# Small matmuls of a hybrid SSD and attention block, put into tiles of the TensorE array

## The chip, the cores and the metric

The kernel runs on one core of one Trainium2 chip. The metric is the time of one execution in microseconds on the device. The kernel before takes 2657.98 us, the median of three runs (2657.9 to 2659.08).

The core's engines run side by side, each through its own list of instructions: TensorE (PE; its weight loads are listed apart as PEld), VectorE (DVE), ScalarE (ACT), GpSimd (POOL) and SyncE (SP), which issues the DMAs. TensorE multiplies a stationary operand of up to 128 rows by 128 columns with a moving one; the product lands in a bank of PSUM. An operand that lies on a part of the 128 partitions uses a part of the array's rows, and an output on a part of the partitions uses a part of its columns.

## The reference

The reference is two blocks of a network, one behind the other. The first (token mixers and a mixture of experts) isn't touched. The second takes 256 tokens with 16 meta tokens ahead of them, 272 in all, through two layers. Cut to what the change touches:

```python
def ssd_mixer(...):                         # 32 heads of 64, 8 groups
    ...
    y = ssd_chunked(xs, dt, a_log, bm, cm) + xs * d_skip[:, None]
    y = y.reshape(bsz, L, D_INNER) * jax.nn.silu(z)
    y = rms_norm(y.reshape(bsz, L, SSD_GROUPS, ...), norm_g...)   # mean square of each of 8 groups
...
def sliding_window_attention(q, k, v, q_norm_g, k_norm_g, sinks):
    q = rotary(rms_norm(q, q_norm_g), pos)  # 16 query heads of 64
    k = rotary(rms_norm(k, k_norm_g), pos)  # 4 key heads
    ...
    probs = jax.nn.softmax(jnp.concatenate([s_meta, s_band, sink], axis=-1), axis=-1)
...
for l in range(2):
    proj = rms_norm(h, norm1_g[l]) @ w_in[l]
    z, xbc, dt_raw, q, k, v, gate_logits = jnp.split(proj, ...)
    y_ssd, y_attn = ssd_mixer(...), sliding_window_attention(...)
    merged = g_ssd * (y_ssd @ w_ssd_down[l]) + g_attn * (y_attn @ w_attn_down[l])
    h = h + merged @ w_o[l]
    h = h + square(relu(rms_norm(h, norm2_g[l]) @ w_mlp_up[l])) @ w_mlp_down[l]
```

## The kernel before

All activations of the second block lie with features on partitions and the 272 tokens along the free dimension; tile kinds `U` (8 x 272 columns) and `Z` (4 x 272) hold them. The last layer drops the 16 meta tokens from its outputs, so there a tile has 256 columns (`n0` is 16) in most places.

`dense` (L1374) multiplies a weight slice of 512 columns by the activations. It loads 1 MB of weights, and for each 256 columns ScalarE casts them into a tile `Y` of the rounded type (the high part) and VectorE subtracts that from the weights into another `Y` (the low part); six `Y` buffers stand in a ring. Three matmuls for each product (high by high, high by low, low by high) go into one of four PSUM banks `pd`; these are the rows `pd<-U,Y` of the profile. Everything else that TensorE does writes one of four banks `pq`, in plain fp32. `evac` reads the banks when the sums are done.

In a layer the order is: B, C, x and z projections, and behind each pair of x and z slices two groups of the SSD (`ssd_group`, L1654, eight groups); the mean squares of y; the k, v and q projections; attention (L1732); then the projections down, the gates, and the MLP. This is the order of the program's text. A scheduler then lays the instructions of each engine in one row, by priority and by its own estimate of when operands are ready: that is how dense matmuls of later projections come to stand between the small ones.

The small matmuls that the change touches:

- **Mean squares** (`stat`, L1493). ScalarE squares a tile of 128 features into one of five buffers `r1`, and a matmul with a table of constants (`sh`, `sy`) of 28 columns adds the sums of one tile into its rows of a 28-row bank. `stat_y` does this for the 16 tiles of y in two halves, `ev_qkv` (L1562) for 2 tiles of k and 8 of q, column by column as `dense` hands them over. `stats` (L1505) makes inverse roots of the 28 rows.
- **Gain rows** (`ynorm`, L1513). A matmul with a column of the identity spreads one of the 28 rows over 128 partitions; four for each half of y.
- **Meta rows of the SSD** (L1711). The 16 meta tokens act on all tokens. For each head a matmul of 16 rows (`xm`, the meta tokens' x by their step, made by ScalarE at L1697) and 64 output columns starts the sum that two matmuls of the masked products (`sg`, `xd`) go on with.
- **Scores** (L1784). For each of 16 heads up to three matmuls: 128 queries by 272 keys, 128 by 144 and, in layer 0, 16 by 16. A head lies on 64 of 128 partitions: even heads in the lower half, odd heads in the upper. Keys that lie in the other half are taken from a swapped copy (`ksw`, tile name `cr`, L1756). Behind each matmul VectorE scales, masks and takes the maximum (L1785); ScalarE takes the exponentials, VectorE divides (L1798 on), three transposes through TensorE follow (L187, operand `cb`), and ScalarE copies their bank into `pT`. Four heads share a transposed tile of meta columns and the products with v (L1816 on).

Of the kernel before, what the change touches and what calls it, by code (L numbers as in the profile page):

```python
# [17 lines left out]
P = 128  # L18
# [18 lines left out]
for _n, _w in (("cos", 272), ("sin", 272), ("cm", 656), ("am", 432), ("perm", 128),  # L37
               ("hsel", 128), ("e16", 16), ("sh", 54), ("sy", 55)):
    C2[_n] = (_o, _o + _w)
    _o += _w  # L40
# [3 lines left out]
def const_tables():  # L44
# [68 lines left out]
    sh, sy = np.zeros((P, 54), f), np.zeros((P, 55), f)  # L113
# [1176 lines left out]
class Block2:  # L1290
# [8 lines left out]

    def c(self, n):  # L1300
        a, b = C2[n]
        return self.cst[:, a:b]
# [71 lines left out]
    def dense(self, w, cols, xh, xl, n0, evac, nk=8, pairs=False):  # L1374
# [6 lines left out]
        for q0 in range(0, nk, 4):  # L1381
# [5 lines left out]
            for c0 in range(0, npc, 256):  # L1387
# [5 lines left out]
                for m, c in enumerate(cols):  # L1393
                    if not (c0 <= c.start - a < c1):
                        continue
                    s = slice(c.start - a - c0, c.stop - a - c0)
                    o = ps[m][: c.stop - c.start, n0:L2]
                    for q in range(4):
                        kk = q0 + q
                        k.mm3(o, hi[:, q, s], lo[:, q, s], xh(kk)[:, n0:], xl(kk)[:, n0:], kk == 0, kk == nk - 1)  # L1400
        if pairs:
# [26 lines left out]
    def layer(self, l, h, n0, r1=None):  # L1428
# [64 lines left out]
        def stat(ps, src, w, first, last, n1):  # L1493
            sq = self.tl([P, L2], "r1", 5)
            k.act(sq[:, n1:], src, AF.Square)
            k.mm(ps[:28, n1:L2], w, sq[:, n1:], start=first, stop=last)

        def stat_y(hf):
            if hf == 0:
                self.ys = k.pq()  # L1500
            for t in range(8):
                g = 20 + 4 * hf + t // 2
                stat(self.ys, xs[hf][:, t, n0:], self.c("sy")[:, 27 - g : 55 - g], hf == 0 and t == 0, hf == 1 and t == 7, n0)

        def stats(ps, n1):  # L1505
            rs, v = self.row()[:28], self.tl([P, L2], "r1", 5)[:28]
            k.ts(v[:, n1:], ps[:28, n1:L2], EPS, ALU.add)
            self.rsqrt(rs[:, n1:], v[:, n1:], [28, L2 - n1])
            return rs
# [3 lines left out]
        def ynorm(hf, rs):  # L1513
# [48 lines left out]
        def ev_qkv(b, n1):  # L1562
            def f(m, ps):
                k.acopy(qkv[b][:, m, n1:], ps[:, n1:])
                if b < 2 or m < 2:
                    if not qs:
                        qs.append(k.pq())
                    r = 8 * b + 2 * m
                    stat(qs[0], ps[:, n1:], self.c("sh")[:, 26 - r : 54 - r], b == 2 and m == 0, b == 1 and m == 3, n1)
                    self.rotary(qkv[b][:, m], prm["qg"] if b < 2 else prm["kg"], prm["qgp"] if b < 2 else prm["kgp"], n1)  # L1570
# [3 lines left out]
        self.dense(w_in, self.cols(7200, 512), xh, xl, 0, ev_qkv(2, 0))  # L1574
        for j in range(2):
            self.dense(w_in, self.cols(6176 + 512 * j, 512), xh, xl, n0, ev_qkv(j, n0))
# [77 lines left out]
    def ssd_group(self, g, B, C, xsv, zt, tk, cs, ncs, ncm, cs_d, prm, n0):  # L1654
# [31 lines left out]
        xm = self.tl([P, 64], "xm", 2)  # L1686
        for j in range(2):
# [34 lines left out]
    def rotary(self, x, g, gp, n0):  # L1722

        k = self.k
        ps = k.pq()
        k.mm(ps[:, n0:L2], self.c("perm"), x[:, n0:])
        t = self.tl([P, L2], "r1", 5)
        k.stt(t[:, n0:], ps[:, n0:L2], gp, self.c("sin")[:, n0:], ALU.mult, ALU.mult)
        k.stt(x[:, n0:], x[:, n0:], g, self.c("cos")[:, n0:], ALU.mult, ALU.mult)
        k.add(x[:, n0:], x[:, n0:], t[:, n0:])  # L1730

    def attention(self, qkv, oh, ol, rs, prm, n0):  # L1732
# [9 lines left out]
        for i, (a, n) in enumerate(tiles):  # L1742
            k.tr(sp[:n, i * 16 : i * 16 + 16], rs[0:16, a : a + n])
        k.ts(qc[:, :32], sp[:, :32], 0.125, ALU.mult)
        if n0 == 0:
            k.ts(qc[:16, 32:48], sp[:16, 32:48], 0.125, ALU.mult)

        kr = [k.pq(), k.pq()]
        for j in range(2):
            for e in range(2):  # L1750
                r = 16 + 2 * j + e
                k.mm(kr[j][64 * e : 64 * e + 64, :L2], k.ident[0:28, r : r + 1].to_broadcast([28, 64]), rs)
# [17 lines left out]
        for kh in range(4):  # L1770
# [3 lines left out]
            for r in range(4):  # L1774
                hq = 4 * kh + r
                pr, e = hq // 2, hq % 2
                rows = slice(64 * e, 64 * e + 64)
                kt = qt(8 + kh // 2)[:] if kh % 2 == e else ksw[:, kh // 2]
                sp = k.pq()
                lg = self.tl([P, 432], "cb", 2)  # L1780
                mx, su, es = (self.tl([P, 3], f"at{x}", 3) for x in range(3))
                for i, (a, n) in enumerate(tiles):
                    o, nk = geo[i]
                    k.mm(sp[:n, o : o + nk], qt(pr)[rows, a : a + n], kt[rows, 0:nk])  # L1784
                    V.tensor_tensor_reduce(out=lg[:n, o : o + nk], in0=sp[:n, o : o + nk], in1=am[:n, o : o + nk],  # L1785
                                           scale=qc[:n, i * 16 + hq : i * 16 + hq + 1], scalar=prm["sink"][:n, hq : hq + 1],
                                           op0=ALU.add, op1=ALU.max, accum_out=mx[:n, i : i + 1])
                parts = ((P, slice(0, 2)),) + (((16, slice(2, 3)),) if n0 == 0 else ())
                for n, c in parts:
                    k.ts(mx[:n, c], mx[:n, c], -1.0, ALU.mult)  # L1790
                    k.act(es[:n, c], mx[:n, c], AF.Exp, bias=prm["sink"][:n, hq : hq + 1])
                for i, (a, n) in enumerate(tiles):
                    o, nk = geo[i]
                    k.act(lg[:n, o : o + nk], lg[:n, o : o + nk], AF.Exp, bias=mx[:n, i : i + 1], accum_out=su[:n, i : i + 1])
                for n, c in parts:
                    k.add(su[:n, c], su[:n, c], es[:n, c])
                    V.reciprocal(su[:n, c], su[:n, c])
                t2 = k.pq()  # L1798
                for i, (a, n) in enumerate(tiles):
                    o, nk = geo[i]  # L1800
                    k.ts(lgm[:n, i, 32 * r : 32 * r + 16], lg[:n, o : o + 16], su[:n, i : i + 1], ALU.mult)
                    if i < 2:
                        k.ts(lg[:n, o + 16 : o + nk], lg[:n, o + 16 : o + nk], su[:n, i : i + 1], ALU.mult)
                        k.tr(t2[:, a - 16 : a - 16 + n], lg[:n, o + 16 : o + 144])
                    if i < 1:
                        k.tr(t2[:, 256:384], lg[:n, o + 144 : o + 272])
                pT = self.tl([P, 384], "pT", 4)
                k.acopy(pT, t2[:, 0:384])
# [152 lines left out]
```

## Time and profile before

| | before |
|---|---|
| median of the runs | 2657.98 us |
| the profiled execution's own time | 2663.16 us |
| its span on the core | 2661.3 us |
| mean granted TensorE clock | 0.971 |
| second block in the span | about 1343 to 2661 us |
| busy: PE, PEld, DVE, ACT | 2487.2, 1786.6, 1398.3, 1068.1 us |

The predictions are made against the profiled execution. Its span is the time from the first to the last instruction on the core; the 1.9 us between span and time lie around it. Times in the trace count from the start of the span. In a row, "out<-in" names the tiles written and read, "128*64 128x272" is the shape of the stationary operand and of the moving one. Every fp32 matmul appears as two records. All matmuls have line L184 or L187 (a transpose), since helpers record them, so they are told apart by their tiles: `r,cst` are mean squares, `row,ident` gain rows, `sm,xm` meta rows, `Z,Z` and `cr,Z` scores, `ident,cb` a softmax's transposes.

### The profile page before, as it was taken

The page shows a single profiled execution, that of the slowest core. Times are in us where ns is not written, and L with a number is a line of the kernel's source. Part 1 is how long each engine was busy: PE and PEld are TensorE (multiplying, and loading weights), DVE is VectorE, ACT ScalarE, POOL GpSimd, SP SyncE. Part 2 cuts the span into 40 slices and gives each one's busy share as a digit, 9 for nine tenths or more (in the row PEclk, how much of TensorE's full clock was granted, in tenths as well). Part 3 has the DMA queues.
Part 4 walks back from the last instruction along what each step waited for, and adds up shares of the span by engine and source line. Part 5 has one row for each costly group of instructions (what it writes and reads, how often), then busy time and mean ns, then how long its engine had stood idle before and what let it go on. Part 6 is the DMA issues. An engine that isn't in the chain of part 4 may idle for free.

```text
span 2661.3 us, 38832 instructions
## 1 busy us (share of the span) xinstructions
PE 2487.2 (93%) x15461; PEld 1786.6 (67%) x15461; DVE 1398.3 (53%) x2910; ACT 1068.1 (40%) x2134; POOL 8.0 (0%) x21
## 2 busy tenths in 40 slices
PE   8979999998777999999879999999998999999999
PEld 7744333334655333333378977899998898789999
DVE  6862222221757222221287876666557887656654
ACT  3421111111532111211158755556454875555654
POOL 0000000000000000000000000000000000000000
PEclk9989999999888999999979999999999999899999
DMA  8489799998636998999855533335553553234553
GB/s 299 154 315 422 322 397 421 421 403 345 198 112 230 421 387 340 421 421 401 340 175 173 163 112 111 112 127 163 175 171 128 184 165 111 97 126 159 175 187 115
DMA packets 189788, 645.17 MB, mean 242 GB/s; under 512 B 21618, under 2 KB 35988, under 8 KB 139556
## 3 DMA queue, kind: packets, MB, share of 16 engines
q1 hardware_dynamic: 189604, 642.66, 64.6%
q8 instruction: 123, 2.02, 0.3%
q14 instruction: 61, 0.50, 0.1%
HBM read 641.49 MB, written 1.12 MB: 241 GB/s over the span
## 4 chain that ended last, share of the span: by engine, by line
PE 47%; DVE 2%; ACT 1%; issue 0%; DMA 0%; ACTq 0%; DVEq 0%
PE pd L184 38%; PE pq L184 7%; PE pq L187 1%; ACT Y L193 1%; DVE Y L196 0%; DVE r L213 0%; ACT r L190 0%; DMA cst<-in_cst 0%; DVE H L196 0%; ACT xd L193 0%; DVE r L196 0%; DVE ln_st L295 0%; DVE lnr_t L196 0%; DVE U L196 0%; DVE cb L209 0%
## 5 line engine op out<-in xcount | busy, mean ns | idle before, releaser
L184 PE MATMUL pd<-U,Y 128*128 128x272 f32 (+1 forms) x7792 | 1030.2, 290 | 15.4 <-ACT U L193 9.2
L184 PEld LDWEIGHTS pd<-U,Y 128*128 128x128 f32 x7792 | 987.2, 190 | 46.2 <-issue 22.3
L196 DVE TENSOR_TENSOR Y<-w,Y 128x1024 fp32r<-128x1024 f32 x344 | 420.1, 1222 | 248.9 <-ACT Y L193 247.4
L184 PE MATMUL pd<-w,H 128*64 128x512 f32 (+1 forms) x2112 | 502.3, 591 | 1.1 <-DMA w<-in_moe_w_up 1.1
L193 ACT CAST Y<-w 128x1024 fp32r<-128x1024 f32 x344 | 360.1, 1047 | 339.9 <-PE pd L184 300.1
L184 PEld LDWEIGHTS pd<-w,H 128*64 128x64 f32 x2112 | 155.8, 138 | 292.4 <-issue 272.0
L184 PE MATMUL pd<-w,m_hT 128*64 128x512 f32 x1040 | 232.6, 596 | 24.4 <-ACT m_hT L193 24.4
L213 DVE SCALAR_TENSOR_TENSOR t4k<-pd,m_gs,t4k 128x512 fp32r<-128x512 f32 x64 | 48.0, 751 | 272.9 <-ACT t4k L190 270.7
L184 PEld LDWEIGHTS pd<-w,m_hT 128*64 128x64 f32 x1040 | 81.5, 137 | 152.8 <-issue 120.5
L190 ACT ACTIVATE t2k<-pd 128x512 f32<-128x512 f32 (+1 forms) x37 | 21.9, 591 | 296.0 <-PE pd L184 296.0
L190 ACT ACTIVATE t4k<-pd,m_gs 128x512 fp32r<-128x512 f32 x64 | 44.0, 687 | 210.3 <-PE pd L184 193.6
L196 DVE TENSOR_TENSOR t2k<-t2k,pd 128x512 f32<-128x512 f32 (+1 forms) x33 | 22.4, 680 | 178.4 <-PE pd L184 178.4
L196 DVE TENSOR_TENSOR H<-H,pq 128x512 f32<-128x512 f32 x132 | 83.9, 681 | 52.5 <-PE pq L184 52.2
L184 PE MATMUL pd<-Xh,H 128*128 128x512 f32 (+1 forms) x320 | 105.2, 400 | 4.0 <-ACT H L193 4.0
L193 ACT COPY m_hT<-pq 128x512 f32<-128x512 f32 (+1 forms) x34 | 19.5, 573 | 218.6 <-PE pq L187 213.7
L190 ACT ACTIVATE H<-pq,m_gb 128x256 f32<-128x256 f32 (+1 forms) x136 | 64.2, 559 | 99.5 <-PE pq L184 79.0
L213 DVE SCALAR_TENSOR_TENSOR t2k<-t2k,pd 128x512 f32<-128x512 f32 (+1 forms) x33 | 22.4, 678 | 150.5 <-ACT t2k L190 150.5
L213 DVE SCALAR_TENSOR_TENSOR r<-pd,cw,r 128x270 f32<-128x270 f32 (+1 forms) x192 | 87.9, 492 | 3.7 <-ACT r L190 2.1
L184 PEld LDWEIGHTS pq<-m_P,H 128*128 128x128 f32 x544 | 73.0, 206 | 25.1 <-issue 19.5
L184 PEld LDWEIGHTS pq<-t4k,m_pgT 128*128 128x128 f32 x256 | 43.7, 188 | 64.9 <-ACT t4k L190 20.3
L184 PE MATMUL pq<-t4k,m_pgT 128*128 128x512 f32 x256 | 80.2, 426 | 6.3 <-DVE t4k L213 6.3
L193 ACT CAST Xh<-w 128x2048 fp32r<-128x2048 f32 (+4 forms) x34 | 57.3, 1690 | 69.7 <-PE pd L184 55.1
(399 smaller groups left out, 2670.9 us busy)
## 6 DMA issues: line engine op xcount, KB each, us to landing
w<-in_moe_w_gate SPq DMA_DIRECT2D x130, 1024.0 KB, 19.9
w<-in_moe_w_down SPq DMA_DIRECT2D x130, 1024.0 KB, 19.8
w<-in_moe_w_up SPq DMA_DIRECT2D x130, 1024.0 KB, 15.7
w<-in_w_in SPq DMA_DIRECT2D x76, 1024.0 KB, 5.1
w<-in_w_mlp_up SPq DMA_DIRECT2D x32, 1024.0 KB, 5.6
w<-in_w_mlp_down SPq DMA_DIRECT2D x32, 1024.0 KB, 5.0
w<-in_w_ssd_down SPq DMA_DIRECT2D x16, 1024.0 KB, 5.8
w<-in_ev_w_in SPq DMA_DIRECT2D x14, 1024.0 KB, 13.0
```

The costliest lines, as they stand in the source:

```text
L184: return self.nc.tensor.matmul(out, l, r, start=start, stop=stop, **kw)
L187: return self.nc.tensor.transpose(out, in_, self.ident[: in_.shape[0], : in_.shape[0]])
L190: return self.nc.scalar.activation(out, in_, func, **kw)
L193: return self.nc.scalar.copy(out, in_)
L196: return self.nc.vector.tensor_tensor(out=out, in0=a, in1=b, op=op)
L213: return self.nc.vector.scalar_tensor_tensor(out=out, in0=a, scalar=s, in1=b, op0=op0, op1=op1)
```

## The change

The edits concern the second block only.

1. Mean squares: `stat4` sums four tiles in four column groups of 32, so that four matmuls write rows 0, 32, 64 and 96 on of one bank. The tables get 60 columns. `dense` gets an argument `whole`, by which all four columns of a k, v or q slice are evacuated together; the k slice has two tiles only, and two matmuls by zeros fill its bank. `stats` works on 128 partitions. The gain rows of y are read from four row groups of 32, each into its own bank, with the evacuations behind all four.
2. The k scales are read from row groups of 32, the q scales are transposed with all 128 rows and gathered by four VectorE operations in place of two. Rotary works on two tiles at a time.
3. Meta rows: two lasting tiles `xmb`, zeroed once, hold the 16-row slices of a head pair block-diagonally, and one matmul of 64 rows and 128 columns does both heads.
4. Scores: the matmuls of two heads stand side by side, each in its half of the rows and its own bank, in a fixed order; then the softmax of both heads, then six transposes, the second head's first, then two copies.

```diff
-        def stat(ps, src, w, first, last, n1):
-            sq = self.tl([P, L2], "r1", 5)
-            k.act(sq[:, n1:], src, AF.Square)
-            k.mm(ps[:28, n1:L2], w, sq[:, n1:], start=first, stop=last)
+        def stat4(ps, srcs, w, first, last, n1):
+
+            sq = []
+            for src in srcs:
+                if src is not None:
+                    sq.append(self.tl([P, L2], "r1", 5))
+                    k.act(sq[-1][:, n1:], src, AF.Square)
+            zero = self.c("sh")[:, 28:60]
+            for m in (3, 2, 1, 0):
+                on = srcs[m] is not None
+                i = k.mm(ps[32 * m : 32 * m + 32, n1:L2], w if on else zero, sq[m if on else 0][:, n1:], start=first, stop=last)
+                if m < 3:
+                    k.tc.keep_in_program_order(i)
...
+            gps = [k.pq() for _ in range(4)]
             for g in range(4):
-                gp = k.pq()
-                r = 20 + 4 * hf + g
-                k.mm(gp[:, n0:L2], k.ident[0:28, r : r + 1].to_broadcast([28, P]), rs[:, n0:])
+                q = slice(32 * g, 32 * g + 32)
+                k.mm(gps[g][:, n0:L2], k.ident[q, 32 * g + hf : 32 * g + hf + 1].to_broadcast([32, P]), rs[q, n0:])
...
-                k.act(xm[r : r + 16, :], v[:16, 0, e], AF.Identity, scale=tk[:16, 0, h0 + e : h0 + e + 1])
+                k.act(xm[r : r + 16, 64 * e : 64 * e + 64], v[:16, 0, e], AF.Identity, scale=tk[:16, 0, h0 + e : h0 + e + 1])
...
-            for e in range(2):
-                r = 32 * (2 * j + e)
-                k.mm(o[e][:, n0:L2], xm[r : r + 16, :], sm[r : r + 16, n0:272], start=True, stop=False)
+            q = slice(64 * j, 64 * j + 64)
+            k.mm(yp[:, n0:L2], xm[q], sm[q, n0:272], start=True, stop=False)
...
-            for r in range(4):
-                hq = 4 * kh + r
...
+            for r0 in (0, 2):
+                sps = [k.pq(), k.pq()]
                 for i, (a, n) in enumerate(tiles):
                     o, nk = geo[i]
-                    k.mm(sp[:n, o : o + nk], qt(pr)[rows, a : a + n], kt[rows, 0:nk])
...
+                    for e in range(2):
+                        hq = 4 * kh + r0 + e
+                        rows = slice(64 * e, 64 * e + 64)
+                        kt = qt(8 + kh // 2)[:] if kh % 2 == e else ksw[:, kh // 2]
+                        ins = k.mm(sps[e][:n, o : o + nk], qt(hq // 2)[rows, a : a + n], kt[rows, 0:nk])
+                        if i or e:
+                            k.tc.keep_in_program_order(ins)
...
+                t2s = [k.pq(), k.pq()]
+                for e in (1, 0):
+                    lg, t2 = lgs[e], t2s[e]
+                    i0 = k.tr(t2[:, 0:128], lg[:, 288:416])
+                    if e == 0:
+                        k.tc.keep_in_program_order(i0)
+                    k.tc.keep_in_program_order(k.tr(t2[:, 128:256], lg[:, 16:144]))
+                    k.tc.keep_in_program_order(k.tr(t2[:, 256:384], lg[:, 144:272]))
```

What the scheduler makes of it is seen in the rows of each engine. Three places follow. The first is TensorE in layer 0, in the second q projection; `pd_...<-U,Y` are dense matmuls, `r,cst` mean squares, `Z,cst` the rotary's permutations. Before:

```order
L184 MATMUL pq_10656<-r_2087_10809,cst_7945 28x272
L184 MATMUL pq_10832<-Z_10533,cst_7945 128x272
L184 MATMUL pq_10656<-r_2090_10819,cst_7945 28x272
L184 MATMUL pd_10838<-U_7961,Y_10844 128x272
L184 MATMUL pd_10838<-U_7962,Y_10844 128x272
L184 MATMUL pd_10838<-U_7961,Y_10845 128x272
L184 MATMUL pd_10838<-U_7961,Y_10844 128x272
L184 MATMUL pd_10838<-U_7962,Y_10844 128x272
L184 MATMUL pq_10656<-r_2093_10829,cst_7945 28x272
L184 MATMUL pd_10838<-U_7961,Y_10845 128x272
```

Now, in the same projection:

```order
L184 MATMUL pd_10820<-U_7965,Y_10827 128x272
L184 MATMUL pq_10809<-Z_10513,cst_7945 128x272
L184 MATMUL pq_10635<-r_2079_10790,cst_7945 32x272
L184 MATMUL pq_10635<-r_2078_10788,cst_7945 32x272
L184 MATMUL pq_10635<-r_2077_10786,cst_7945 32x272
L184 MATMUL pq_10635<-r_2076_10784,cst_7945 32x272
L184 MATMUL pq_10808<-Z_10513,cst_7945 128x272
L184 MATMUL pd_10820<-U_7965,Y_10826 128x272
```

Mean squares that stood one by one between dense matmuls stand four together. Counted over both layers, 52 of them in 30 places became 14 fours.

The second place is TensorE in the attention of layer 0, at the scores of one head before (`Z,Z`; the 272-key matmul stands 14 rows ahead of the first row here):

```order
L184 MATMUL pd_11970<-U_10498,Y_12059 128x272
L184 MATMUL pq_11287<-Z_10532,Z_10533 128x144
L184 MATMUL pd_11970<-U_10499,Y_12059 128x272
L184 MATMUL pd_11970<-U_10498,Y_12060 128x272
L184 MATMUL pd_11970<-U_10498,Y_12059 128x272
L184 MATMUL pd_11970<-U_10499,Y_12059 128x272
L184 MATMUL pd_11970<-U_10498,Y_12060 128x272
L184 MATMUL pq_11287<-Z_10532,Z_10533 16x16
L184 MATMUL pd_11970<-U_10498,Y_12059 128x272
```

Now, the scores of a pair behind the transposes of the pair ahead:

```order
L184 MATMUL pd_11953<-U_10478,Y_11986 128x272
L187 MATMUL pq_11293<-ident,cb_11269 128x128 x3
L187 MATMUL pq_11292<-ident,cb_11246 128x128 x3
L184 MATMUL pq_11304<-cr_11053,Z_10513 128x272
L184 MATMUL pq_11305<-Z_10512,Z_10513 128x272
L184 MATMUL pq_11304<-cr_11053,Z_10513 128x144
L184 MATMUL pq_11305<-Z_10512,Z_10513 128x144
L184 MATMUL pq_11304<-cr_11053,Z_10513 16x16
L184 MATMUL pq_11305<-Z_10512,Z_10513 16x16
L184 MATMUL pd_11953<-U_10478,Y_11985 128x272
```

The scores of a head were spread over three places with dense matmuls between; those of two heads are one run now. Between a pair's scores and its transposes 42 to 51 dense matmuls stand in layer 0 and 42 to 54 in layer 1.

The third place is ScalarE in the attention of layer 0: the exponentials of one head before (`at` and `cb` are a head's small and large tiles, `Y` a cast of weights, `U` an evacuation):

```order
L193 COPY U_11726<-pd_11730 128x272
L190 ACTIVATE at_2172_11199<-at_2170_11197,sk_7666 128x2
L190 ACTIVATE cb_11196,at_2171_11198<-cb_11196,at_2170_11197 128x272
L190 ACTIVATE cb_11196,at_2171_11198<-cb_11196,at_2170_11197 128x144
L190 ACTIVATE at_2172_11199<-at_2170_11197,sk_7666 16x1
L190 ACTIVATE cb_11196,at_2171_11198<-cb_11196,at_2170_11197 16x16
L193 CAST Y_12059<-w_12029 128x1024
L193 COPY pT_11226<-pq_11217 128x384
```

Now, those of a pair:

```order
L190 ACTIVATE at_2177_11249<-at_2175_11247,sk_7666 128x2
L190 ACTIVATE cb_11246,at_2176_11248<-cb_11246,at_2175_11247 128x272
L190 ACTIVATE at_2177_11249<-at_2175_11247,sk_7666 16x1
L190 ACTIVATE cb_11246,at_2176_11248<-cb_11246,at_2175_11247 128x144
L190 ACTIVATE cb_11246,at_2176_11248<-cb_11246,at_2175_11247 16x16
L190 ACTIVATE at_2181_11272<-at_2179_11270,sk_7666 128x2
L190 ACTIVATE at_2181_11272<-at_2179_11270,sk_7666 16x1
L190 ACTIVATE cb_11269,at_2180_11271<-cb_11269,at_2179_11270 128x272
L190 ACTIVATE cb_11269,at_2180_11271<-cb_11269,at_2179_11270 128x144
L190 ACTIVATE cb_11269,at_2180_11271<-cb_11269,at_2179_11270 16x16
L193 COPY U_11710<-pd_11714 128x272
L193 CAST Y_12015<-w_12013 128x1024
```

The exponentials of both heads stand together, and the casts of weights behind them.

More of the change, by code (lines that the diff above doesn't have):

```diff
@@ L1298, in __init__ @@
         k.nc.gpsimd.memset(self.k1024, 1.0 / 1024)
+        self.xmb = [big.tile([P, P], F32, name=f"xmb{i}", tag=f"xmb{i}", bufs=1) for i in range(2)]
+        for t in self.xmb:
+            k.nc.gpsimd.memset(t, 0.0)
     def c(self, n):
@@ L1372, in rsqrt, with dense @@
             k.stt(y, t, 1.5, y, ALU.add, ALU.mult)
-    def dense(self, w, cols, xh, xl, n0, evac, nk=8, pairs=False):
+    def dense(self, w, cols, xh, xl, n0, evac, nk=8, pairs=False, whole=False):
         k = self.k
@@ L1400, in dense @@
                         k.mm3(o, hi[:, q, s], lo[:, q, s], xh(kk)[:, n0:], xl(kk)[:, n0:], kk == 0, kk == nk - 1)
+        if whole:
+            evac(0, [p[:, :L2] for p in ps])
+            return
         if pairs:
@@ L1500, in stat_y @@
                 self.ys = k.pq()
[L1501 to L1503 removed]
+            for u in range(2):
+                stat4(self.ys, [xs[hf][:, 2 * g + u, n0:] for g in range(4)], self.c("sy")[:, 27 - hf : 59 - hf],
+                      hf == 0 and u == 0, hf == 1 and u == 1, n0)
         def stats(ps, n1):
[L1506 to L1508 removed]
+            rs, v = self.row(), self.tl([P, L2], "r1", 5)
+            k.ts(v[:, n1:], ps[:, n1:L2], EPS, ALU.add)
+            self.rsqrt(rs[:, n1:], v[:, n1:], [P, L2 - n1])
             return rs
@@ L1562, in ev_qkv, with f @@
         def ev_qkv(b, n1):
[L1563 to L1570, printed above, removed]
+            def f(_, ps):
+                if not qs:
+                    qs.append(k.pq())
+                n = 4 if b < 2 else 2
+                for m in range(4):
+                    k.acopy(qkv[b][:, m, n1:], ps[m][:, n1:])
+                stat4(qs[0], [ps[m][:, n1:] if m < n else None for m in range(4)],
+                      self.c("sh")[:, 26 - 2 * b : 58 - 2 * b], b == 2, b == 1, n1)
+                g, gp = (prm["qg"], prm["qgp"]) if b < 2 else (prm["kg"], prm["kgp"])
+                for m in range(0, n, 2):
+                    self.rotary([qkv[b][:, m], qkv[b][:, m + 1]], g, gp, n1)
             return f
-        self.dense(w_in, self.cols(7200, 512), xh, xl, 0, ev_qkv(2, 0))
+        self.dense(w_in, self.cols(7200, 512), xh, xl, 0, ev_qkv(2, 0), whole=True)
         for j in range(2):
-            self.dense(w_in, self.cols(6176 + 512 * j, 512), xh, xl, n0, ev_qkv(j, n0))
+            self.dense(w_in, self.cols(6176 + 512 * j, 512), xh, xl, n0, ev_qkv(j, n0), whole=True)
         rs = stats(qs[0], 0)
@@ L1742, in attention @@
         for i, (a, n) in enumerate(tiles):
[L1743 to L1746, printed above, removed]
+            k.tr(sp[:n, i * P : (i + 1) * P], rs[:, a : a + n])
+        qv = qc.rearrange("p (i b m e) -> p i b m e", i=3, b=2, m=4)
+        sv = sp[:, : 3 * P].rearrange("p (i m x) -> p i m x", i=3, m=4)
+        for b in range(2):
+            k.ts(qv[:, 0:2, b], sv[:, 0:2, :, 2 * b : 2 * b + 2], 0.125, ALU.mult)
+            if n0 == 0:
+                k.ts(qv[:16, 2, b], sv[:16, 2, :, 2 * b : 2 * b + 2], 0.125, ALU.mult)
         kr = [k.pq(), k.pq()]
@@ L1789, in attention @@
[L1789 to L1806, printed above, removed]
@@ new lines, in attention @@
+                t2s = [k.pq(), k.pq()]
[6 more added lines that the diff above has]
+                    k.tc.keep_in_program_order(k.tr(t2[:, 256:384], lg[:, 144:272]))
+                for e in range(2):
+                    pT = self.tl([P, 384], "pT", 4)
+                    k.acopy(pT, t2s[e][:, 0:384])
+                    pts.append(pT)
```

68 lines of the change are left out of this document (43 added, 25 removed).

## The prediction, made before the run

> **What bounds the kernel now.** I read the page first, then busy time by stretches of the second block, then the TensorE groups by shape, and last the time line of the places that the change touches. The first rows are the busy time of TensorE over the span and the engines' shares of the chain that ended last.
>
> ```profile
> PE 2487.2 (93%) x15461; PEld 1786.6 (67%) x15461; DVE 1398.3 (53%) x2910; ACT 1068.1 (40%) x2134; POOL 8.0 (0%) x21
> ...
> PE 47%; DVE 2%; ACT 1%; issue 0%; DMA 0%; ACTq 0%; DVEq 0%
> ```
>
> The chain is TensorE's own. The change edits only the second block, so I asked for the two stretches of layer 0 where its operations lie: the end of the SSD groups with the q and k projections, and the attention. The columns are length, then busy time of PE, PEld, DVE, ACT and POOL, the granted clock, and the DMA share with its rate.
>
> ```profile
> 1540.00:1630.00 90.00, 88.71 (x568) 67.65 (x567) 63.74 (x132) 46.65 (x109) 0.84 (x2) 0.99 0.28 92
> 1630.00:1770.00 140.00, 140.00 (x970) 117.10 (x970) 84.68 (x309) 80.45 (x215) 0.84 (x2) 0.98 0.36 119
> ```
>
> TensorE does not rest for one microsecond of the attention, while VectorE and ScalarE are busy for 85 and 80 of 140 us. So every microsecond of matmul time saved here shortens the span, until a softmax or an evacuation comes late. That is the frame of the sum: what TensorE no longer does, less the waits that the new order makes.
>
> **Mean squares.** Each fp32 matmul leaves two records. The 104 records below are 52 matmuls of 28 columns that sum squares over partitions.
>
> ```profile
> L184 PE MATMUL pq<-r,cst 128*28 128x272 f32 x56 | 16.1, 399 | 0.0
> L184 PE MATMUL pq<-r,cst 128*28 128x256 f32 x48 | 12.6, 384 | 0.0
> ```
>
> The time line (start, length) shows what one costs in a row of its kind, and what it costs between dense matmuls.
>
> ```profile
> 1544.03 3.85 PE L184 MATMUL pq<-r,cst 128*28 128x272 f32 x16
> 1547.81 0.73 PE L184 MATMUL pq<-Z,bm 128*128 128x272 f32 x2
> ...
> 1564.68 0.64 PE L184 MATMUL pq<-r,cst 128*28 128x272 f32 x2
> 1565.25 8.03 PE L184 MATMUL pd<-U,Y 128*128 128x272 f32 x62
> 1573.32 2.07 PE L184 MATMUL pq<-row,ident 28*128 28x272 f32 x8
> 1575.32 0.64 PE L184 MATMUL pq<-r,cst 128*28 128x272 f32 x2
> ```
>
> Eight in a row take 1547.81 - 1544.03 = 3.78 us, 0.47 each. One alone takes 0.57 to the next start. A dense matmul takes 8.03 / 62 = 0.130. To this comes a toll for leaving the dense stream, which the scores show:
>
> ```profile
> 1668.80 0.72 PE L184 MATMUL pq<-Z,Z 64*128 64x272 f32 x2
> 1669.46 2.01 PE L184 MATMUL pd<-U,Y 128*128 128x272 f32 x14
> 1671.40 0.51 PE L184 MATMUL pq<-Z,Z 64*128 64x144 f32 x2
> 1671.84 0.89 PE L184 MATMUL pd<-U,Y 128*128 128x272 f32 x5
> 1672.66 0.21 PE L184 MATMUL pq<-Z,Z 64*16 64x16 f32 x2
> 1672.80 0.77 PE L184 MATMUL pd<-U,Y 128*128 128x272 f32 x4
> ```
>
> Fourteen dense matmuls between two scores take 1.94 us against 14 x 0.130 = 1.82, and five take 0.82 against 0.65. I take 0.15 us a trip. In the order of before, the 52 matmuls stand in 30 trips: 30 x (0.57 + 0.15) + 22 x 0.47 = 31.9 us. After, 14 quads of four are left (per layer four for y, one for k, two for q). If a quad's four column groups work side by side it costs one trip and 0.05 for the starts: 14 x 0.77 = 10.8. Less 0.6 for layer 1's shorter tiles, the gain is 20.5 us. If they go one behind the other, a quad costs 0.72 + 3 x 0.47 + 0.05 = 2.18, and the gain is only 1.4.
>
> The trace of before has no quad, but it has halves: matmuls of 64 output columns with their pair.
>
> ```profile
> 1658.52 0.67 PE L184 MATMUL pq<-sm,xd 16*64 16x272 f32 x4
> 1659.12 0.87 PE L184 MATMUL pq<-pT,xd 128*64 128x256 f32 x8
> 1659.92 0.67 PE L184 MATMUL pq<-sm,xd 16*64 16x272 f32 x4
> ```
>
> Two 272-column matmuls take 0.60 us, what one mean square alone takes; the four behind them (two of 256 and two of 128 columns) take 0.80. So column halves do run together, and I take the quad nearer to that than to a serial one. A quad also needs eight weight loads, of which the nearest row is
>
> ```profile
> 1551.62 0.63 PEld L184 LDWEIGHTS pq<-sg,xd 128*64 128x64 f32 x8 [0.41 <-DVE sg L196]
> ```
>
> eight in 0.63 us, while the matmuls of the same tiles streamed from 1551.63 on. The Trainium skill, page "TensorE: Matmul & The Clock Gate", section "The mechanism", says that a weight load overlaps matmuls in flight only when its row group differs; the four column groups of a quad share all rows, so it speaks against this part. The row disagrees for column halves; by the rule the quads would gain 8.8 us less, 14 x 0.63.
>
> **Scores.** From the rows above one head costs 0.66 + 0.44 + 0.14 us and three trips, 1.69 us, in layer 0, and 1.40 in layer 1, which has no 16-row part: 16 x 1.69 + 16 x 1.40 = 49.4 us. After, two heads go in one trip, six matmuls in three pairs of row halves. Side by side a pair costs the 1.24 us of one head and one toll at most, and 1.1 to 1.2 where the later ones shrink like the mean squares in a row. I take 1.3 and 1.1: 8 x 1.3 + 8 x 1.1 = 19.2, a gain of 30.2 us. Row halves with all 128 columns have no row in the trace: if they are serial, the second head adds 0.47 + 0.25 + 0.06 us in layer 0 and 0.72 in layer 1, 12.0 in all, and the gain is 18.2.
>
> **Meta rows.** Two 16-row matmuls per head pair become one of 64 rows.
>
> ```profile
> 1451.66 1.24 PE L184 MATMUL pq<-sm,xm 16*64 16x272 f32 x6
> 1452.83 0.87 PE L184 MATMUL pq<-sg,xd 128*64 128x256 f32 x8
> 1453.63 0.67 PE L184 MATMUL pq<-sm,xm 16*64 16x272 f32 x2
> 1454.23 0.73 PE L184 MATMUL pq<-Z,bm 128*128 128x272 f32 x2
> ```
>
> They cost 1.17 + 0.60 = 1.77 us a group now. The new ones could take 0.67, but ScalarE feeds them late:
>
> ```profile
> 1451.22 1.29 ACT L190 ACTIVATE xm<-pq,tk 16x64 f32<-16x64 f32 x4
> ```
>
> The first new matmul needs two of these four slices and the second needs all. The last slice ends at 1452.51, 0.85 us behind the place where the first matmul stands now, and the second matmul takes some 0.7 more: 1.56 us, so 0.21 is gained in each of 16 groups, 3.4 us. Where the slices come early the gain is 1.1, 17.6 in all. I take 5, near the row. The two tiles with their zeros are written once, by GpSimd, whose 8.0 us of work in the page's first row leave it free.
>
> **Gain rows.** The four broadcasts at 1573.32 take 2.00 us; from four row groups, about 0.65, once in each layer: 2.7. Those of the second half stay scattered. I count nothing for the q scales, whose extra two VectorE operations have its idle time as cover. Gains: 20.5 + 30.2 + 5 + 2.7 = 58.4 us.
>
> **What the new order costs.** Now the two heads' softmax must end before six transposes, and only dense matmuls cover it. The chain, from rows of one head:
>
> ```profile
> 1694.69 0.72 PE L184 MATMUL pq<-Z,Z 64*128 64x272 f32 x2
> ...
> 1695.58 0.55 DVE L1785 CUSTOM_DVE_ANT_0 cb<-pq,cst,sk 128x272 f32<-128x272 f32 x1
> 1697.21 0.42 DVE L1785 CUSTOM_DVE_ANT_0 cb<-pq,cst,sk 128x144 f32<-128x144 f32 x1 [1.07 <-PE pq L184]
> 1698.18 0.28 DVE L1785 CUSTOM_DVE_ANT_0 cb<-pq,cst,sk 16x16 f32<-16x16 f32 x1 [0.32 <-PE pq L184]
> ...
> 1700.45 0.16 DVE L196 TENSOR_TENSOR at<-at,at 128x2 f32<-128x2 f32 x1
> 1701.72 0.22 DVE L209 TENSOR_SCALAR sg<-cb,at 16x16 f32<-16x16 f32 x1
> ...
> 1699.04 0.47 ACT L190 ACTIVATE at<-at,sk 128x2 f32<-128x2 f32 x2
> 1700.53 0.18 ACT L190 ACTIVATION_READ_ACCUMULATOR cb<-cb,at 16x1 f32 x1
> ```
>
> The first reduction starts 0.89 us behind its score. The three of a head, 1.25 us, with their readouts and sign changes make about 1.6; both heads 3.2. From ScalarE's first exponential of the last head to VectorE's last product it is 1701.94 - 1699.04 = 2.90. Sum 7.0 us in layer 0. Without the 16-row parts, 0.4 us a head on VectorE and some 0.6 behind them, it is about 5.6. The cover is the trip itself plus 42 to 51 dense matmuls in layer 0, 1.3 + 42 x 0.130 = 6.8 to 7.9 us, and 6.4 to 8.1 in layer 1 by the same spacing. The two casts and products of weights that stood inside a head's chain now stand behind the pair's. So layer 0 is just covered: I take 3 us for 16 pairs, from 0 to 16.8 (one cast of 1.05 us inside each).
>
> At the start of attention TensorE already waits:
>
> ```profile
> 1627.69 0.93 PE L184 MATMUL pq<-Z,Z 64*128 64x272 f32 x2 [1.20 <-ACT xd L193]
> ...
> 1627.66 1.70 ACT L193 COPY cr<-Z 64x272 f32<-64x272 f32 x4
> ```
>
> The second head of the first pair needs the swapped copy of k, which ends at 1629.36, so the pair's trip is 1.7 us later in layer 0; for layer 1, with fewer rows to copy, I take 1.0: 2.7 us. The k and q evacuations now come four columns at a time and hold the four dense banks together: 1 us, between 0 and 3. Costs: 3 + 2.7 + 1 = 6.7.
>
> **Sum.** 58.4 - 6.7 = 51.7 us. The profiled execution took 2663.16, so 2611.5; the median of the runs, 2657.98, lies 5.18 lower: 2606. The bounds of the small terms (meta rows 3.4 to 17.6, waits 2.7 to 22.5) are not all met at once; its own range is 2595 to 2622.
>
> **The rivals.** *Serial tiles*: quads and score pairs do not overlap, gains 1.4 + 18.2 + 5, costs the same, 17.9 net: 2640. Against it stand the 0.60 us of two column halves; for it, that no row shows quarters or full-width row halves. 0.10. *Exposed loads*: 8.8 less gain, 2615; against it the load row. 0.08. *More gain*: no pair waits, no evacuation waits, slices early: 51.7 + 3 + 1 + 12.6 = 68.3, 2590. 0.09. *Covered in part*: a cast in every chain, 13.8 more than I took, 2620; cast and product (1.23 us more each), 2640. 0.08. *Slower*: a wait draws the clock down. After the 1.20 us wait that ended at 1627.69 the trace has
>
> ```profile
> 1628.00:1635.00 7.00, 7.00 (x28) 5.64 (x27) 3.58 (x15) 6.44 (x20) 0.00 (x0) 0.51 0.47 152
> ...
> 2053.40:2060.00 6.60, 4.65 (x38) 4.60 (x37) 6.14 (x11) 5.63 (x8) 0.00 (x0) 1.00 0.32 95
> ```
>
> seven microseconds at clock 0.51, about 3.4 us lost. If each pair waits 1.2 us and then runs at half clock, 16 x 4.6 = 73.6 in place of 3: 2677. It decides from 12 of the 16 pairs, since without pair waits 54.7 us are gained. For it: layer 0's cover is 0.2 us short at its least. Against it: the second row, 1.95 us idle in 6.60 at full clock, and layer 1's longer cover. The waits for a softmax are short now:
>
> ```profile
> PE pq L187 <- DVE cb L209: 1.4, 5, 0.3
> ```
>
> five, none above 0.3 us. 0.05. The page named above, in "Why this matters for your kernels", puts the limit at gaps of about 3 us, by which 1.2 us would draw nothing; the first row has a drop behind a wait of 1.20.
>
> **How the numbers follow.** The forecast has 0.60. The range, 2588 to 2642, takes in all cases but the slower one and a little beyond. Faster by over 0.2% (5.3 us, about what a measurement can tell) 0.92; within it 0.03, the worst of the partly covered; slower 0.05.
>
> **What would show it.** Right: the mean squares as quads of about 0.6 us between dense matmuls, six scores in about 1.2 us, pair transposes with waits under 0.5 us, a first pair that waits about 3 us. Wrong: quads of 2 us, weight loads with gaps between them, waits of over a microsecond at every pair's transposes, or half-clock stretches inside the attention.

## The result, and the profile after

The changed kernel takes 2601.11 us (2599.17 to 2601.43, four runs) against 2658.47 (2657.9 to 2659.08, four runs): a ratio of 0.9778, with a 95% interval of 0.9765 to 0.979. That is 57.4 us less by the medians and 59.0 by the ratio. The forecast was 2606, 52 us less than the median it started from.

The profiled execution took 2601.37 us, with a span of 2599.6 and a mean clock of 0.972. It is 61.8 us shorter than the profiled execution before, which lay 4.7 us above the median of its kernel. First the same rows of the page as before.

```profile
PE 2422.4 (93%) x15405; PEld 1762.8 (68%) x15405; DVE 1391.0 (54%) x2913; ACT 1062.8 (41%) x2134; POOL 8.3 (0%) x23
...
PE 35%; DVE 2%; ACT 2%; issue 1%; ACTq 0%; DVEq 0%
```

TensorE's busy time fell by 64.8 us, VectorE's and ScalarE's by 7.3 and 5.3: the time went where the forecast looked for it. The chain that ended last is still TensorE's own, though it is followed back less far, 40% of the span. The next rows are the end of layer 0's SSD groups with the k and q projections, and its attention, by busy time of PE, PEld, DVE, ACT and POOL, clock, and DMA.

```profile
1535.00:1618.00 83.00, 80.18 (x581) 65.47 (x579) 64.34 (x138) 48.29 (x112) 0.84 (x2) 0.98 0.33 108
1618.00:1740.00 122.00, 121.69 (x975) 111.45 (x975) 81.31 (x308) 76.81 (x212) 0.84 (x2) 0.99 0.41 133
```

TensorE still rests for only 0.3 us of the attention, though VectorE and ScalarE now carry the same softmax in less time (VectorE is busy for 81 of 122 us, before for 85 of 140).

**Mean squares.** Two quads of the time line, TensorE's matmuls first, then the weight loads of the first quad.

```profile
1557.02 0.67 PE L184 MATMUL pq<-r,cst 128*32 128x272 f32 x8
1557.61 1.76 PE L184 MATMUL pd<-U,Y 128*128 128x272 f32 x12
1559.31 0.67 PE L184 MATMUL pq<-r,cst 128*32 128x272 f32 x8
1559.90 7.66 PE L184 MATMUL pd<-U,Y 128*128 128x272 f32 x59
```

```profile
1557.01 0.16 PEld L184 LDWEIGHTS pq<-r,cst 128*32 128x32 f32 x8 [0.15 <-issue]
```

Four matmuls take 0.59 us to the next start, where one took 0.57 before. All eight loads are done in 0.16 us, at the head of the quad.

**Scores.** The transposes of one pair, the scores of the next, and the transposes that end its softmax.

```profile
1644.29 0.85 PE L187 MATMUL pq<-ident,cb 128*128 128x128 f32 x6
1645.07 0.49 PE L184 MATMUL pq<-cr,Z 64*128 64x272 f32 x1
1645.07 0.49 PE L184 MATMUL pq<-Z,Z 64*128 64x272 f32 x1
...
1646.01 0.17 PE L184 MATMUL pq<-cr,Z 64*16 64x16 f32 x1
1646.02 0.17 PE L184 MATMUL pq<-Z,Z 64*16 64x16 f32 x1
1646.12 6.16 PE L184 MATMUL pd<-U,Y 128*128 128x272 f32 x47
1652.29 0.85 PE L187 MATMUL pq<-ident,cb 128*128 128x128 f32 x6
```

The two heads' matmuls start together and the pair takes 1.05 us, from 1645.07 to 1646.12. In layer 1 a pair takes 0.90. The first pair of each layer is the exception: its second head starts late and the clock is at half, and it takes 3.12 and 2.55 us. The chain that this pair's transposes waited for, on VectorE and then on ScalarE:

```profile
1644.38 2.36 DVE L196 TENSOR_TENSOR Y<-w,Y 128x1024 fp32r<-128x1024 f32 x2
1646.66 0.56 DVE L1819 CUSTOM_DVE_ANT_0 cb<-pq,cst,sk 128x272 f32<-128x272 f32 x1
...
1648.66 0.28 DVE L1819 CUSTOM_DVE_ANT_0 cb<-pq,cst,sk 16x16 f32<-16x16 f32 x1
...
1651.88 0.27 DVE L209 TENSOR_SCALAR cb<-cb,at 128x128 f32<-128x128 f32 x1
```

```profile
1650.95 0.19 ACT L190 ACTIVATION_READ_ACCUMULATOR cb<-cb,at 16x1 f32 x1
1651.04 1.98 ACT L193 CAST Y<-w 128x1024 fp32r<-128x1024 f32 x2
```

From the first score to the last product that a transpose reads it is 1652.15 - 1645.07 = 7.08 us; the cover of 1.05 and 47 dense matmuls ends at 1652.2. The first reduction starts 1.59 us behind its score, not 0.89, since VectorE is still at two operations on weights (`Y<-w,Y`); the two heads' reductions then take 2.5 us, not 3.2. What TensorE waited for in the second block (total, times, longest), the four largest of the 14 rows among those that lie where the change does:

```profile
PE pq L187 <- ACT xd L193: 1.5, 1, 1.5
...
PE pq L184 <- DVE U L213: 1.2, 2, 0.7
PE pq L187 <- DVE cb L209: 1.2, 5, 0.4
PE pq L187 <- DVE qc L209: 0.8, 1, 0.8
```

The softmax is waited for five times, for 1.2 us together; before it was five times and 1.4. The waits for `U`, at the mean squares, and for `qc`, the q scales of layer 1, are new; `xd`, at the start of attention, was waited for twice before, for 2.4 us together.

**Meta rows.** The two block-diagonal matmuls of a group, and the last three of ScalarE's four slices for them.

```profile
1514.22 1.31 PE L184 MATMUL pq<-sm,xmb 64*128 64x272 f32 x4
1515.45 0.87 PE L184 MATMUL pq<-sg,xd 128*64 128x256 f32 x8
```

```profile
1513.80 0.95 ACT L190 ACTIVATE xmb<-pq,tk 16x64 f32<-16x64 f32 x3
```

They take 1.23 us: the second starts 0.58 behind the first, at 1514.80, and the last slice ends at 1514.75.

**Clock.** The stretch at half clock at the start of attention is still there, behind a wait of 1.53 us now; in the rest of the attention, with its short waits, there is none.

```profile
1613.50:1621.50 8.00, 7.83 (x37) 6.35 (x37) 5.41 (x26) 7.23 (x27) 0.00 (x0) 0.57 0.37 131
1621.50:1740.00 118.50, 118.19 (x958) 107.95 (x957) 77.86 (x289) 73.55 (x196) 0.84 (x2) 1.00 0.41 134
```

**The account.** I took, in both traces from 1343 us on, the time from each matmul record's start to the next one's, without idle time, and added it up by tile.

| | before, us | after, us | difference |
|---|---|---|---|
| mean squares | 26.6 | 8.2 | -18.4 |
| `Z,Z` and `cr,Z` (scores, and some of the SSD's) | 48.9 | 30.2 | -18.7 |
| dense `pd` | 1064.9 | 1051.1 | -13.8 |
| meta rows | 25.7 | 19.7 | -6.0 |
| gain rows and k scales | 11.8 | 7.8 | -4.0 |
| softmax transposes | 13.9 | 11.6 | -2.3 |
| rotary | 8.9 | 7.6 | -1.3 |
| idle | 22.8 | 26.1 | +3.3 |
| all, with the rest | | | -61.3 |

A part of this is the clock: half of the matmul time inside stretches at half clock is 17.7 us before and 14.0 after, so 3.7 of the 61.3 us, and 4.4 of the 13.8 in the dense rows, come from there. (The trace of before has one such stretch more, at 2276 us, behind no wait; one in layer 1 is shorter there than after.) The dense matmuls are as many as before; the other 9.4 us that they lost are the toll of the trips. TensorE leaves a run of dense matmuls 168 times before and 105 times after, which makes 0.15 us a trip. The scores and their transposes have 64 trips fewer. The mean squares have 11 fewer (18 before, 7 after), but the rotary's matmuls, which often stood next to them, now leave the dense stream 13 times in place of 4, so that hardly any trip is saved there.

### The profile page after: what moved, and what is told of

Its sections match the earlier page's. It is cut to its first block, busy times and chain, and to the rows that moved or that the text cites. A ratio compares the mean times of both kernels' runs of the same rounds, so it can differ in the third digit from the quotient of the medians.

```text
span 2599.6 us, 38742 instructions
## 1 busy us (share of the span) xinstructions
PE 2422.4 (93%) x15405; PEld 1762.8 (68%) x15405; DVE 1391.0 (54%) x2913; ACT 1062.8 (41%) x2134; POOL 8.3 (0%) x23
## 5 line engine op out<-in xcount | busy, mean ns | idle before, releaser
L184 PE MATMUL pd<-U,Y 128*128 128x272 f32 (+1 forms) x7792 | 1011.2, 288 | 15.8 <-ACT U L193 9.2
L184 PEld LDWEIGHTS pq<-t4k,m_pgT 128*128 128x128 f32 x256 | 43.6, 187 | 64.8 <-ACT t4k L190 20.3
```

Source lines behind the costliest of these rows:

```text
L184: return self.nc.tensor.matmul(out, l, r, start=start, stop=stop, **kw)
```

## The experiments

The theory after the result: the gain is TensorE time alone. It has two sources, matmuls that run side by side on parts of the array and trips out of the dense stream that fall away, and the parts of the change add up. The rivals are that the parts help one another, that the trips alone or the overlap alone make the gain, and for the meta rows that matmuls of 64 rows can't overlap there. Every kernel was timed against the kernel before on the same chip, whose median was 2660.13, 2659.85 and 2659.89 us in the three rounds of experiments. Savings in us are worked out from the ratio; the medians differ from them by up to 1 us.

**Mean squares alone.** The kernel before with `stat4`, the gain rows, the scales, `whole` and rotary in pairs; of the diff, all but the scores' loop and the `xmb` tiles.

```diff
-            k.mm(ps[:28, n1:L2], w, sq[:, n1:], start=first, stop=last)
+                i = k.mm(ps[32 * m : 32 * m + 32, n1:L2], w if on else zero, sq[m if on else 0][:, n1:], start=first, stop=last)
```

> Only the mean squares in quads, the gain rows from row groups, the k and q scales and the evacuation of four columns together; scores and meta rows as before. If the parts add up as worked out, the time falls by 21 to 25 us (30 places become 14 and a quad takes about 0.6 us), to about 2635. If the quads drew their gain from the other parts (less waiting on banks or on ScalarE because of the paired scores), it falls by clearly less, 10 to 15 us. If side by side were worth nothing it would fall by about 4.

Measured: 2638.48 us, ratio 0.9915 (0.9901 to 0.9929), 22.6 us less. The part stands by itself.

**Scores alone.** The kernel before with the pairs' loop only.

```diff
-            for r in range(4):
+            for r0 in (0, 2):
+                sps = [k.pq(), k.pq()]
```

> Only the paired scores with their softmax and transposes; mean squares and meta rows as before. If the parts add up, it falls by 28 to 33 us, to about 2628. The rival in which pair softmaxes are waited for gives 15 to 20, with waits of TensorE for the large softmax tile at the transposes of over half a microsecond.

Measured: 2628.38 us, ratio 0.9877 (0.9862 to 0.9892), 32.7 us less. No pair softmax is waited for at length.

**Meta rows alone.**

```diff
-        xm = self.tl([P, 64], "xm", 2)
+        xm = self.xmb[g % 2]
...
+            k.mm(yp[:, n0:L2], xm[q], sm[q, n0:272], start=True, stop=False)
```

> Only the block-diagonal meta rows. If ScalarE's slices hold the second matmul back, it falls by 4 to 7 us, to about 2653, and the two matmuls of a group start 0.6 us apart. If both run side by side it falls by 15 to 18.

Measured: 2652.83 us, ratio 0.9973 (0.9962 to 0.9983), 7.2 us less, with an interval of 4.5 to 10.1. Some of it is probably the clock: four of its eight executions had a mean clock of 0.975 and took 2650.23 to 2651.17 us, the other four 0.972 or 0.973 and 2654.49 to 2656.55. The three parts make 62.5 us by their ratios, the whole change 59.0 by its own, with an interval of 56 to 62: they add up within what is measured.

**Mean squares in all 128 columns.** Nothing side by side, only no partial array.

```diff
-               ("hsel", 128), ("e16", 16), ("sh", 54), ("sy", 55)):
+               ("hsel", 128), ("e16", 16), ("sh", 154), ("sy", 155)):
...
-            k.mm(ps[:28, n1:L2], w, sq[:, n1:], start=first, stop=last)
+            k.mm(ps[:, n1:L2], w, sq[:, n1:], start=first, stop=last)
```

> The kernel before, with the mean squares' table widened by zeros so that each matmul uses all 128 columns; one tile at a time, nowhere in quads. If a matmul on part of the array costs more between dense ones just because it is on a part (0.80 us beyond the dense ones for 28 columns, 0.46 for the rotary's full 128 by 128), 30 places save 0.34 each: it falls by 8 to 12 us, to about 2648. If only working side by side counts, it stays at 2658 within 2 us. If leaving the partial array is the whole gain of the quads, it falls by 20 or more.

Measured: 2653.21 us, ratio 0.9974 (0.9964 to 0.9985), 6.9 us less, with an interval of 4 to 9.6: a little under what was expected, and not nothing. The time line shows the place that took 0.57 us with 28 columns:

```profile
1562.15 0.73 PE L184 MATMUL pq<-r,cst 128*128 128x272 f32 x2
1562.51 8.12 PE L184 MATMUL pd<-U,Y 128*128 128x272 f32 x62
```

The next dense matmul starts after 0.36 us: behind a matmul of all 128 columns the dense stream goes on sooner than behind one of 28. Why, no run shows. By the account the mean squares lose 4.0 us this way; as quads they lose 18.4.

**Runs of four in the same columns.** The order of the quads without the overlap: the kernel before, with the mean squares in runs of four (two for the k slice).

```diff
-            k.mm(ps[:28, n1:L2], w, sq[:, n1:], start=first, stop=last)
+                i = k.mm(ps[:28, n1:L2], ws[m], sq[m][:, n1:], start=first and m == n - 1, stop=last and m == 0)
```

> The kernel before, with the mean squares gathered in runs of mostly four as in the changed kernel, but all four in the same 28 columns, so that they can't run side by side; gain rows, scales, scores and meta rows as before, q and k evacuated four columns together. By the price in a row (0.47 us each) against 0.72 for one alone, some 13 trips fewer save about 3 us and the rotary's pairs 1: ratio about 0.9985. If fewer trips made most of the quads' gain, it falls by 12 us or more: 0.9955 or less.

Measured: 2655.27 us, ratio 0.9981 (0.9972 to 0.999), 5.1 us less. A run of four takes 1.95 us to the next start:

```profile
1560.63 2.02 PE L184 MATMUL pq<-r,cst 128*28 128x272 f32 x8
1562.58 0.64 PE L184 MATMUL pd<-U,Y 128*128 128x272 f32 x3
```

against the quad's 0.59. By the account the mean squares take 24.8 us here and 8.2 as quads: the 16.6 us between them are the overlap. The trips can't have given the 5.1 us. TensorE leaves the dense stream 173 times here, no less often than before, since the rotary's matmuls leave it in the squares' place. A part is probably the clock: its mean is 0.975 in this run and 0.973 in the kernel before, and the two executions of this run at 0.973 took 2657.66 and 2658.28 us.

**Head after head.** The changed kernel with the loop over heads outside.

```diff
-                for i, (a, n) in enumerate(tiles):
-                    o, nk = geo[i]
-                    for e in range(2):
+                for e in range(2):
+                    for i, (a, n) in enumerate(tiles):
+                        o, nk = geo[i]
```

> The changed kernel, but the scores of a pair go head after head (three of the first, then three of the second) in the same run, so that hardly any two matmuls in opposite row halves meet; trips, softmax and transposes stay. If side by side is worth what the sum said, 12 us come back (0.78 and 0.72 us a pair): ratio to before about 0.9825. If the whole gain of the scores is the saved trips, it stays at the changed kernel's 0.978 within 0.001.

Measured: 2609.38 us, ratio 0.9807 (0.9793 to 0.982), some 8 us above the changed kernel and less than the 12 expected. The trace says why. Layer 0's pairs:

```profile
1638.47 1.11 PE L184 MATMUL pq<-cr,Z 64*128 64x272 f32 x6
1639.51 1.11 PE L184 MATMUL pq<-Z,Z 64*128 64x272 f32 x6
1640.55 0.39 PE L184 MATMUL pd<-U,Y 128*128 128x272 f32 x1
```

take 2.08 us, one head and then the other; seven of the eight are like this, and the first, at half clock, is 0.27 us longer than in the changed kernel. That makes 7.5 us. Layer 1's:

```profile
2264.01 0.49 PE L184 MATMUL pq<-Z,Z 64*128 64x272 f32 x1
2264.03 0.49 PE L184 MATMUL pq<-cr,Z 64*128 64x272 f32 x1
...
2264.58 0.28 PE L184 MATMUL pq<-Z,Z 64*128 64x144 f32 x1
2264.59 0.28 PE L184 MATMUL pq<-cr,Z 64*128 64x144 f32 x1
...
2264.93 0.39 PE L184 MATMUL pd<-Z,Y 128*128 128x256 f32 x1
```

overlap as before, 0.91 us, though the second head's first matmul (`cr,Z`, 272 columns) stands in the list behind the first head's 144-column one: it starts 0.013 us behind the head of the run, and 0.55 ahead of its predecessor. The two layers differ in the 16 by 16 matmuls that end a head in layer 0. So this run takes the overlap away in layer 0 only, and no run prices it in layer 1. For the scores neither source makes the gain alone: of 32.7 us, layer 0's overlap is 7.5, and 64 trips at 0.15 us are 9.6. Why the two layers differ was a new question, and the next run put it.

**Head after head, the short ones last.**

```diff
+                for e, i in ((0, 0), (0, 1), (1, 0), (1, 1), (0, 2), (1, 2))[: 2 * len(tiles)]:
+                        (a, n), (o, nk) = tiles[i], geo[i]
```

> Head after head as in the earlier run, but the two 16 by 16 score matmuls of layer 0 stand at the end of the pair's run. There the pairs of layer 0 took 2.08 us and those of layer 1, which have no 16-row part, 0.91, as short as side by side. If what stops the overlap is the change of the stationary operand's shape (64*128 to 64*16 and back) between the heads, layer 0's pairs fall back to 1.05 to 1.2 us and the ratio to the changed kernel's 0.978. If it is the head-after-head order itself, they stay near 2.0 us and the ratio at 0.981.

Measured: 2601.7 us, ratio 0.9781 (0.9767 to 0.9794), that of the changed kernel. Layer 0's pairs, where the first head's 144-column matmul again stands ahead of the second head's first:

```profile
1636.51 0.49 PE L184 MATMUL pq<-cr,Z 64*128 64x272 f32 x1
1636.53 0.49 PE L184 MATMUL pq<-Z,Z 64*128 64x272 f32 x1
...
1637.57 0.39 PE L184 MATMUL pd<-U,Y 128*128 128x272 f32 x1
```

take 1.06 us. So what stopped the overlap was the 16 by 16 matmul between the heads, and not the order of the heads. It differs from the others in the shape of its stationary operand, 64*16. But it also puts the second head three matmuls behind the first in place of two, and TensorE may reach ahead only so far. A place in the first block bears on this, here in the trace of before:

```profile
718.09 1.71 PE L184 MATMUL pq<-t2k,t2k 64*128 64x128 f32 x16
```

Four matmuls of one row half stand ahead of four of the other, all of one shape. By the starts of the single records the fifth starts 0.55 us behind the first, together with the third and ahead of the fourth, so the reach there was two matmuls. By such a reach alone, the second head would have started with the 144-column matmul, 0.56 us behind the first, and a part of the pair would have overlapped. It started after 1.04 us, behind all of the first head, which speaks for the shape.

**Meta slices in time.** The changed kernel with the second pair's slices first and both matmuls together.

```diff
-        for j in range(2):
+        for j in (1, 0):
             t = 2 * g + j
...
+        yps = [k.pq(), k.pq()]
+        for j in range(2):
+            q = slice(64 * j, 64 * j + 64)
+            i = k.mm(yps[j][:, n0:L2], xm[q], sm[q, n0:272], start=True, stop=False)
+            if j:
+                k.tc.keep_in_program_order(i)
```

> The changed kernel, with the second head pair's meta slices made first and the two meta matmuls issued one right behind the other, when all four slices are there. If the slices hold the second matmul back (0.60 to 0.65 us between the two starts in ten of the twelve groups where they stand together), both now run side by side, a group's pair takes about 0.7 us in place of 1.3, and 7 to 9 us go: ratio about 0.975. If two 64-row matmuls with all 128 columns can't run together here, or the later first matmul costs what it saves, it stays at 0.978.

Measured: 2598.22 us, ratio 0.9765 (0.9751 to 0.9778). That is 3 us by the medians, at the edge of the intervals, and not 7 to 9.

```profile
1514.89 0.73 PE L184 MATMUL pq<-sm,xmb 64*128 64x272 f32 x4 [0.37 <-ACT xmb L190]
1515.55 0.87 PE L184 MATMUL pq<-sg,xd 128*64 128x256 f32 x8
```

The two do overlap: 0.63 to 0.66 us for the pair, in all 16 groups, and the account gives 9.4 us less for the meta rows. But TensorE now waits for the last slice ahead of them, 0.3 to 0.5 us in 14 groups, and the idle time of the second block is 7.8 us more. The slices held the second matmul back, and now they hold both.

**Slices by two engines.** Only that VectorE makes every other slice.

```diff
+                if e:
+                    k.ts(xm[r : r + 16, 64 * e : 64 * e + 64], v[:16, 0, e], tk[:16, 0, h0 + e : h0 + e + 1], ALU.mult)
```

> The changed kernel, with half of the meta slices (one head of each pair) made by VectorE, beside ScalarE's. If the slices hold the matmuls back, each pair of slices is there 0.33 us earlier, and 2 to 5 us go, less what VectorE's 32 more operations delay: ratio about 0.977. If the slices don't matter it stays at 0.978 or gets slower.

Measured: 2599.82 us, ratio 0.9772 (0.9759 to 0.9785): not told apart from the changed kernel, whose meta rows (19.7 us) became 20.4. The run does not test the slices: in its trace the two matmuls of a group stand together in none of the 16 groups, so that they had no chance to overlap. In the changed kernel they stood together in 12.

**Both, and full gain rows.** The two edits, and the second half's gain rows with all 128 rows.

```diff
+                q = slice(32 * g, 32 * g + 32) if hf == 0 else slice(0, P)
+                k.mm(gps[g][:, n0:L2], k.ident[q, 32 * g + hf : 32 * g + hf + 1].to_broadcast([q.stop - q.start, P]), rs[q, n0:])
```

> Both of these edits, and the second half's gain rows, which stand one by one between dense matmuls, by matmuls of all 128 rows. By the price of a full matmul between dense ones (0.46 us beyond them against 0.80 for a partial one) the eight gain rows give 2 to 3 us more: ratio about 0.974. If the terms do not add, it stays with the best of the others.

Measured: 2591.51 us, ratio 0.9742 (0.9728 to 0.9755), as expected, and the best kernel here: 9.6 us under the changed one.

```profile
1505.84 0.73 PE L184 MATMUL pq<-sm,xmb 64*128 64x272 f32 x4
1506.50 1.52 PE L184 MATMUL pq<-sg,xd 128*64 128x256 f32 x16
```

The pair takes 0.66 us, and only two of the 16 groups have a wait of over 0.25 us ahead of it, where 14 had one with ScalarE's slices alone. By the account the meta rows lose 9.4 us against the changed kernel, the gain rows 2.3, and idle time grows by 1.9. The slice edits gave 3 us or less one by one; two matmuls that need all slices at once pay only if the slices come in time.

## Why the prediction was right

The frame held: TensorE was the chain, and the time that it saved left the span. The forecast's net 51.7 us came out as 57.4.

- **Mean squares and gain rows.** 20.5 and 2.7, less 1 for the evacuation, were forecast; this part alone gave 22.6. The choice between a quad near the halves' price and a serial one was right, 0.59 us against the 0.62 taken without the trip, and the run of four in the same columns shows that this choice carried the term. That the total fits so closely is partly luck. The mean squares gave 18.4 us in the account, since the toll of 0.15 us for each of 16 trips was not saved; the gain rows with the k scales gave 4.0, and the rotary 1.3 that the sum did not have.
- **Exposed loads.** The rule of the Trainium skill, page "TensorE: Matmul & The Clock Gate", section "The mechanism", that loads overlap only across row groups, would have cost 8.8 us. Eight loads of a quad, all on the same rows, took 0.16 us together, and the quad no more than a single matmul. The trace doesn't agree with the rule here.
- **Scores.** 30.2 less the 5.7 of waits, 24.5, were forecast; alone they gave 32.7. A pair takes 1.05 and 0.90 us and a toll of 0.15, against 1.3 and 1.1 taken; the first pairs, at 3.12 and 2.55, use this up. The larger miss is the waits. The term that was mis-sized is "I take 3 us for 16 pairs": the softmax waits did not grow. For the pair shown, the chain was 7.08 us, as the sum of 7.0 said, but by luck, since two of its terms were off by 0.7 us each way (1.59 for 0.89, 2.5 for 3.2). The scheduler had laid 47 dense matmuls there, and the two met within 0.1 us.
- **Start of attention.** "2.7 us" was mis-sized too. TensorE waits 1.53 and 0.17 us in layer 0, where it waited 1.20, and 0.77 us in layer 1, where it waited 1.20.
- **Meta rows.** 5 taken, 7.2 measured alone, 6.0 in the account. The reason given, that slices at 0.33 us hold the second matmul back, is what the runs showed: with the slices of both ahead of them, the pair went from 1.23 to 0.66 us.
- **Serial tiles.** The rival for 2640 falls: quads and pairs run side by side. For the pairs the trace of before could have told. The prediction says that row halves with all 128 columns have no row there, but the first block has one, two matmuls of one half and then two of the other:

```profile
52.03 1.14 PE L184 MATMUL pq<-H,H 64*128 64x256 f32 x8
```

By the starts of the single records the second half's first matmul starts 0.014 us behind the first half's, ahead of that half's second.

- **Slower.** It needed waits of over a microsecond at 12 of 16 pairs; the longest wait for a softmax tile was 0.4 us, and none drew the clock down.

By its terms the forecast was 2.5 us short in the gains (60.9, the account without idle and without the clock's 3.7) and 3.4 us too dear in the waits (6.7 against 3.3).

## What to carry to other kernels

Where TensorE is the chain, look for its small matmuls between large ones and price each by the distance between starts, with the trip, not by its length: here a matmul of 28 columns cost as much as four side by side. Count the trips of everything that stands there, since a trip is saved only if nothing else takes its place. Put the matmuls that are ready together into tiles of the array of one shape, since here one of another shape between two heads went with the loss of their overlap. Make sure that all their operands come in time, or the gain turns into a wait. Before counting a softmax or another long chain as a loss, count what the scheduler has laid over it.

## What was not expected of the hardware

- Matmuls in opposite row halves overlapped even when issued head after head: the second head's first started 0.013 us behind the first head's first, though another matmul of the first head stood between in the list. The Trainium skill, page "TensorE: Matmul & The Clock Gate", section "The mechanism", has matmuls start strictly in the order of issue; the starts in this record don't.
- One 16 by 16 matmul between two heads cost an overlap of 1.03 us a pair, more than the matmul itself takes (about 0.14 us). That the change of the stationary operand's shape did it is likely by the traces, but no run changed the shape alone.
- Half-clock stretches of about 7 us followed waits of 1.20 and 1.53 us at the start of attention, while one of 1.95 us in layer 1 drew none in the 6.6 us looked at, and one came at 2276 us in the kernel before behind no wait. With the meta rows alone the same wait of 1.20 us, in layer 0, drew none either:

```profile
1622.00:1630.00 8.00, 6.18 (x41) 4.85 (x39) 4.89 (x16) 7.53 (x22) 0.00 (x0) 1.00 0.41 131
```

The clock, the third number from the end, stays at 1.00. The length of the wait alone doesn't decide, then; what does stays open.
